# Seven products in another order: a product into another bank between two into the same one

## The chip, the cores and the metric

The kernel runs on one core of a Trainium2 chip. The metric is the device time of one launch in microseconds, lower is better. The kernel before was run three times: median 2225.44 us, from 2217.04 to 2226.3. One further execution was profiled; it took 2224.22 us, of which the profile's span, first to last instruction, is 2222.5 us.

## What is computed

One layer of a causal encoder on 2048 tokens of width 1024, in float32: a gated linear attention mixer (4 heads, keys of 128, values of 256, chunks of 64), then a feed-forward block with a causal convolution of width 3, then a last normalization.

```python
# mixer
h = rmsnorm(x, mix_norm_w)
q, k, v, r, glr = split(h @ gla_w_in, [512, 1024, 2048, 3072])
log_a = log_sigmoid(glr @ w_gate2 + b_gate) / 16
g = cumsum(log_a within a chunk);  k_dec = k * exp(g_end - g)
state = state * exp(g_end) + k_dec^T v        # a scan over 32 chunks
o = q @ state
o = rms_normalize(o) * gla_norm_w * silu(r)
x = x + o @ gla_w_out
# feed-forward
h = rmsnorm(x, ffn_norm_w)
g, val = split(causal_dwconv(h @ ffn_w_up, conv_w, conv_b))
x = x + (silu(g) * val) @ ffn_w_down
out = rmsnorm(x, final_norm_w)
```

Every product is made in three matmuls of a high and a low half (high x low, low x high, high x high), so that float32 accuracy is kept; mm3p (lines 172 to 182) writes these three, at lines 177, 178 and 179.

## The kernel before

The large products are not done block by block but by a Strassen-Winograd scheme: a product of 2 x 2 blocks (two row tiles of 128 tokens, two halves of the inner dimension, two blocks of 512 columns) is made of seven products p1 to p7 of sums and differences of blocks, instead of eight. A product is 4 x 3 = 12 matmuls of 128 x 128 by 128 x 512.

The mixer's projections run as four sweeps over the eight pairs of row tiles, one after another: R (the gate r, and the small gate product glr beside it), A and B (keys, queries and values of heads 0, 1 and of heads 2, 3) and Y (the output projection). One pair in one sweep is a unit (function unit, line 1045). In A and B, and in Y's first two units, the scan of the pairs before runs in between: scan_f, scan_k, scan_o and scan_x are called at fixed places among a unit's 28 quarter products (SLOTS, SLOTS_END, lines 724 to 726). After Y come U, the up projection (phase_u, line 1174) with the order OPS, and D, the down projection (line 1333), with an order of its own.

PSUM has eight banks: four for products (mm_ps, line 124), four for transposes, scan and others (aux_ps, line 127). In a unit, three products begin a bank: p1, p5 and p2. p6, p7 and p4 are added into p1's bank one after another, p3 into p5's. What the bank holds between two of them is also a result: after p1, p5 and p6 ScalarE copies it out (line 1128, tiles cp); after p7, p2 and p3 VectorE adds a copy to it (line 1072, tiles o22, o11, o12); after p4 it is copied out (R, line 1144) or split into halves straight from the bank (A and B, scan_v, line 626). In Y VectorE adds the bank into the residual x after each product (line 1117). A product that is added into a bank can start only when the bank has been read after the product before it.

The weights of a sweep (sums and differences of four blocks of a weight matrix, in high and low halves) lie in seven buffers, one for each product; during the last unit of a sweep each is overwritten with the next sweep's weight, at due times that the kernel keeps on a clock of its own (plan_w, line 326). For A the blocks are loaded into a ring of four raw buffers and added up on VectorE (sum_w, line 286; WPLAN, line 319, gives due times); for B and Y the sums were made and stored before. In Y's last unit the buffers are filled with U's operands instead (load_op, line 882, four loads of 512 KB each on SP's queue). The row operands are split two products ahead (prep_rows, LEAD = 2; tiles h_R, h_A, h_B, h_Y); in R they come from transposed and subtracted blocks in a ring of buffers (hb_tile, line 381; diff, line 384), and R stores them for A and B.

The order is one tuple for sweeps and U alike:

```python
OPS = PORD = ("p1", "p5", "p6", "p7", "p4", "p2", "p3")
```

The code's order is the order of issue that the framework starts from. The framework's scheduler sets the final order of each engine's queue and the semaphores.

Of the kernel before, what the change touches and what calls it, by code (L numbers as in the profile page):

```python
# [10 lines left out]
F32 = mybir.dt.float32  # L11
# [5 lines left out]
P = 128  # L17
# [8 lines left out]
def hybrid_kernel(  # L26
# [17 lines left out]
    nc = tc.nc  # L44
# [11 lines left out]
    NTT = S // P  # L56
# [27 lines left out]
    NS = S // TS  # L84
    TT = TS // P
    PAIRS = TT // 2
    OPS = PORD = ("p1", "p5", "p6", "p7", "p4", "p2", "p3")
    NQ = NF // 2
    ULEAD = 5
    DLEAD = 4  # L90
# [147 lines left out]
    wgot, wload = {}, {}  # L238
# [47 lines left out]
    def sum_w(ps_, o, k):  # L286

        v, r = raws_of(ps_, o, k)
        src = xsum[v]
        if o == "p5":  # L290
            nc.vector.tensor_add(src, *r)
        elif o == "p6":
            nc.vector.tensor_sub(src, src, r[0])
        elif o == "p7":
            nc.vector.tensor_sub(r[1], *r)
        elif o == "p3":
            r = wgot[ps_, "p2", k, (0, 1)]
            nc.vector.tensor_sub(src, r, src)

    def split_w(ps_, o, k):  # L300
        if k == 0:
            t = uh.tile([P, KT, 512], F32R, tag=o, name=f"w_{ps_}_{o}", bufs=1)
            W[ps_, o] = t[:, :HK, :], t[:, HK:, :]
        hi, lo = W[ps_, o]
        if (ps_, o, k) in wgot:
            v, src = (slice(None), slice(2 * k, 2 * k + 2)), wgot[ps_, o, k]
            split(hi[v], lo[v], src)
            if k == 1:
                ready.add((ps_, o))
            return  # L310
        v, r = raws_of(ps_, o, k)
        src = {"p5": xsum[v], "p6": xsum[v], "p3": xsum[v]}.get(o, r[-1] if r else None)
        split(hi[v], lo[v], src)
        if k == 1:
            ready.add((ps_, o))
# [2 lines left out]

    WPLAN = (
# [4 lines left out]
    )  # L324

    def plan_w(ps_):
        def do(o, n):
            if o is None:
                load_w(ps_, n)
                return  # L330
            if o in WSUM:
                sum_w(ps_, o, n)
            split_w(ps_, o, n)

        plan = WPLAN
        if ps_ in "BY":
            plan = [(MADE0 + MADE * m, PORD[m // 2], m % 2) for m in range(2 * len(PORD))]
            for m in range(2 * len(PORD)):
                heapq.heappush(wevents, (clock["now"] + MADE0 + MADE * (m + 0.4), next(seq), lambda m=m: load_made(ps_, m + 1 + RB)))
        for us, o, n in plan:  # L340
            fn = (lambda o=o, n=n: do(o, n)) if ps_ == "A" else (lambda o=o, n=n: split_w(ps_, o, n))
            heapq.heappush(wevents, (clock["now"] + us, next(seq), fn))
        if ps_ == "Y":
            def first_x():
                load_made(ps_, 2 * len(PORD))
                for t in range(2):
                    xin[t] = load_x(t, "x1")

            heapq.heappush(wevents, (clock["now"] + 25.5, next(seq), first_x))
# [15 lines left out]
    rp = {}  # L365
    hsrc = {}
# [12 lines left out]
        nc.vector.scalar_tensor_tensor(xt, xt, rstd, rp["nw"], op0=ALU.mult, op1=ALU.mult)  # L379

    def hb_tile(name):
        return rp["h"].tile([P, 512], F32, tag="hb", name=name, bufs=7)

    def diff(j, o, a, c):
        d = hb_tile(f"ht_{j}_{o}")
        nc.vector.tensor_sub(d, a, c)
        hsrc[j, o] = d
        return d
# [37 lines left out]
    def prep_row(ps_, j, o):  # L426
        if ps_ == "R":
            need(f"h{j}")
            if o == "p4":
                diff(j, o, *hsrc.pop(("p4", j)))  # L430
            split_row(ps_, j, o, hsrc.pop((j, o)))
        else:
            m = jobs.index((ps_, j, o))
            for n in range(m, min(m + HB - 1, len(jobs))):
                if jobs[n] not in hraw:
                    p_, j_, o_ = jobs[n]
                    hraw[jobs[n]] = row_tile(f"hr_{p_}{j_}_{o_}")
                    nc.sync.dma_start(hraw[jobs[n]], (yd if p_ == "Y" else h1d)[j_, o_])
            split_row(ps_, j, o, hraw.pop((ps_, j, o)))
# [181 lines left out]
    def scan_e(g, t):  # L621
        e = sp["a"].tile([P, 2 * DK], F32, tag="E", name=f"E_{g}_{t}", bufs=2)
        nc.sync.dma_start(e, ed[t][:, 2 * g * DK:2 * (g + 1) * DK])
        return e
# [420 lines left out]
    def unit(ps_, j):  # L1045
# [33 lines left out]
        for i, o in enumerate(PORD):  # L1079
# [31 lines left out]
            if ps_ == "Y":  # L1111
                while d not in xin:
                    heapq.heappop(wevents)[-1]()
                xe, xd = xin[e], xin[d]
                for xt, cs in {"p1": ((xe, c1),), "p5": ((xd, c2),), "p6": ((xd, c1),), "p2": ((xe, c1),),
                               "p7": ((xd, c2),), "p3": ((xd, c1),), "p4": ((xe, c2),)}[o]:
                    add(xt[:, cs], xt[:, cs], a)
                if o in ("p2", "p3"):
                    t, xt = (e, xe) if o == "p2" else (d, xd)
                    held.append((t, xt))  # L1120
                if j < 2:
                    scan_slot(4 * i + 4)
                while held and not scan:
                    x1_done(*held.pop(0))
                continue
# [9 lines left out]
            if ps_ == "R":  # L1135
                if o == "p2":
                    nc.sync.dma_start(rd[e][0], o11)
                elif o == "p7":
                    nc.sync.dma_start(rd[d][1], o22)
                elif o == "p3":  # L1140
                    nc.sync.dma_start(rd[d][0], o12)
                elif o == "p4":
                    o21 = out_tile(f"o21_{ps_}_{j}")
                    nc.scalar.copy(o21, a)
                    nc.sync.dma_start(rd[e][1], o21)
            else:
                if o == "p7":
                    if j == 0 and g == 0:
                        scan_a()
                    n = NTT * g + e  # L1150
                    scan[n] = {"g": g, "t": e, "e": scan_e(g, e)}
                    scan[n + 1] = {"g": g, "t": d, "v": scan_v(g, d, o22)}
                elif o == "p4":
                    scan[n]["v"] = scan_v(g, e, a)
                elif o == "p2":
                    if j == 0 and g == 0:
                        scan_b()
                    scan[n]["kq"] = o11
                elif o == "p3":
                    scan[n + 1].update(kq=o12, e=scan_e(g, d))  # L1160
                scan_slot(4 * i + 4)


# [390 lines left out]
```

## Time and profile before

| | |
|---|---|
| median of three runs | 2225.44 us |
| the profiled execution | 2224.22 us, span 2222.5 us |
| granted TensorE clock, mean | 0.986 |
| TensorE matmuls / weight loads | busy 95% / 78% |
| VectorE / ScalarE / GpSimd | busy 74% / 50% / 33% |
| DMA | 411.78 MB, mean 185 GB/s |
| sweep R from 53.6 us, A from 241.2, B from 463.8, Y from 698.8 to 893.7 | 187.6, 222.6, 235.0, 194.9 us |

In the profile a row of a group of instructions names line, engine, operation and tiles (out<-in), and its times. PE is TensorE's matmuls and PEld its weight loads, DVE VectorE, ACT ScalarE, POOL GpSimd, SPq the queue of SyncE that issues most DMAs. The tiles mp_R, mp_A, mp_B and mp_Y are the product banks of the four sweeps. The end of a matmul is modelled, so the distance between starts tells more than the durations.

### The profile page before, as it was taken

What the parts mean: (1) busy time and instruction counts of PE and PEld (TensorE: products, weight loads), DVE (VectorE), ACT (ScalarE), POOL (GpSimd) and SP (SyncE); (2) the same over time, 40 slices, a digit from 0 to 9 for tenths busy, and PEclk for the clock granted to TensorE, in tenths of its full rate; (3) what the DMA queues carried; (4) which work ended last, traced back from release to release, by engine and by line L of the source; (5) the groups of instructions that cost most, each with busy time, mean ns of one, the idle gap of its engine ahead of it and who ended that gap; (6) DMA issues with size and microseconds to landing.
All of it is one profiled execution on the core that took longest, in us unless ns stands there. A gap on an engine that the chain in (4) does not pass through costs nothing.

```text
span 2222.5 us, 29090 instructions
## 1 busy us (share of the span) xinstructions
PE 2122.4 (95%) x9952; PEld 1743.6 (78%) x9952; DVE 1636.5 (74%) x2167; ACT 1107.9 (50%) x2024; POOL 733.1 (33%) x602
## 2 busy tenths in 40 slices
PE   6999999989998999898999999999999999999998
PEld 5888787877887787677887777788888887888886
DVE  8655787789778765488899786897877777457564
ACT  5554755565556676444555453454554443333342
POOL 1000011111111000355566664656555435036100
PEclk9999999999999999999999999999999999999999
DMA  6645684478557889935435348433332468354453
GB/s 210 218 165 182 203 264 157 131 223 299 164 161 235 283 321 352 315 117 174 155 120 193 105 139 288 142 112 102 103 111 85 159 243 289 128 180 152 142 176 113
DMA packets 305125, 411.78 MB, mean 185 GB/s; under 512 B 23742, under 2 KB 160110, under 8 KB 304976
## 3 DMA queue, kind: packets, MB, share of 16 engines
q1 hardware_dynamic: 267440, 346.99, 47.2%
q10 hardware_dynamic: 37536, 62.93, 8.4%
q8 instruction: 78, 1.28, 0.2%
q14 instruction: 71, 0.58, 0.1%
HBM read 266.70 MB, written 143.13 MB: 184 GB/s over the span
## 4 chain that ended last, share of the span: by engine, by line
PE 62%; DVE 14%; DMA 9%; issue 7%; ACT 3%; POOL 3%; SPq 1%; ACTq 0%; DVEq 0%; POOLq 0%
PE ua L177 5%; PE pd_p L178 5%; PE pd_p L179 5%; PE pd_p L177 5%; PE ua L179 5%; PE ua L178 5%; DVE t L1237 4%; PE uc L177 2%; PE uc L179 2%; PE uc L178 2%; PE mp_R L177 2%; PE mp_R L179 2%; PE mp_R L178 2%; PE mp_Y L177 2%; PE mp_Y L179 2%
## 5 line engine op out<-in xcount | busy, mean ns | idle before, releaser
L177 PE MATMUL ua<-h_p,uw_p 128*128 128x512 f32 x704 | 280.2, 398 | 23.6 <-ACT c L1219 23.6
L178 PE MATMUL ua<-h_p,uw_p 128*128 128x512 f32 x704 | 278.6, 396 | 0.0
L179 PE MATMUL ua<-h_p,uw_p 128*128 128x512 f32 x704 | 278.4, 395 | 0.0
L1237 DVE SCALAR_TENSOR_TENSOR t<-u,cw,t 128x1024 f32<-128x1024 f32 x176 | 263.3, 1500 | 8.9 <-ACT t L1235 7.9
L178 PE MATMUL pd_p<-dw_p,da 128*128 128x512 f32 x616 | 240.5, 390 | 3.1 <-DVE da L187 3.1
L179 PE MATMUL pd_p<-dw_p,da 128*128 128x512 f32 x616 | 240.1, 390 | 0.0
L177 PE MATMUL pd_p<-dw_p,da 128*128 128x512 f32 x616 | 240.1, 390 | 0.0
L187 DVE TENSOR_TENSOR uw_p<-ur,uw_p 128x512 fp32r<-128x512 f32 x176 | 168.3, 972 | 58.5 <-ACT uw_p L186 53.3
L187 DVE TENSOR_TENSOR da<-da_p,da 128x512 fp32r<-128x512 f32 x154 | 133.6, 920 | 105.4 <-ACT da L186 105.3
L186 ACT CAST da<-da_p 128x512 fp32r<-128x512 f32 x154 | 85.2, 619 | 208.9 <-PE pd_p L179 153.3
L177 PEld LDWEIGHTS ua<-h_p,uw_p 128*128 128x128 f32 x704 | 134.1, 191 | 57.2 <-ACT c L1219 27.6
L186 ACT CAST uw_p<-us 128x512 fp32r<-128x512 f32 x132 | 82.1, 622 | 165.8 <-POOL us L1199 108.3
L187 DVE TENSOR_TENSOR uw_p<-us,uw_p 128x512 fp32r<-128x512 f32 x132 | 120.4, 921 | 57.6 <-ACT uw_p L186 57.2
L179 PEld LDWEIGHTS ua<-h_p,uw_p 128*128 128x128 f32 x704 | 134.0, 190 | 30.1
L178 PEld LDWEIGHTS ua<-h_p,uw_p 128*128 128x128 f32 x704 | 134.3, 191 | 29.5
L177 PE MATMUL uc<-h_p,uw_p 128*128 128x512 f32 x352 | 138.3, 393 | 1.0 <-DVE t L1237 1.0
L179 PE MATMUL uc<-h_p,uw_p 128*128 128x512 f32 x352 | 138.0, 392 | 0.0
L178 PE MATMUL uc<-h_p,uw_p 128*128 128x512 f32 x352 | 138.0, 392 | 0.0
L178 PEld LDWEIGHTS pd_p<-dw_p,da 128*128 128x128 f32 x616 | 116.0, 188 | 28.0 <-DVE da L187 3.9
L1235 ACT ACTIVATE t<-u,cw 128x1024 f32<-128x1024 f32 x88 | 109.8, 1247 | 51.2 <-DVE u L1328 43.3
L179 PEld LDWEIGHTS pd_p<-dw_p,da 128*128 128x128 f32 x616 | 116.0, 188 | 24.2
L177 PEld LDWEIGHTS pd_p<-dw_p,da 128*128 128x128 f32 x616 | 115.9, 188 | 24.0
(269 smaller groups left out, 5476.2 us busy)
## 6 DMA issues: line engine op xcount, KB each, us to landing
ur<-in_ffn_w_up_dram SPq DMA_DIRECT2D x168, 256.0 KB, 3.7
da_p<-ad_p SPq DMA_DIRECT2D x154, 256.0 KB, 4.1
h_p<-hd_p SPq DMA_DIRECT2D x56, 512.0 KB, 8.1
ad_p<-as_p SPq DMA_DIRECT2D x88, 256.0 KB, 2.7
ad_p<-t SPq DMA_DIRECT2D x66, 256.0 KB, 3.5
x<-in_x_dram SPq DMA_DIRECT2D x32, 512.0 KB, 4.3
ch<-in_ffn_w_down_dram SPq DMA_DIRECT2D x61, 256.0 KB, 4.4
hr_A_p<-h1d_p SPq DMA_DIRECT2D x56, 256.0 KB, 2.7
```

The lines of the kernel that those rows point to most:

```text
L177: nc.tensor.matmul(ps_ap, ah, bl, start=(first and i == 0), stop=False, **kw)
L178: nc.tensor.matmul(ps_ap, al, bh, start=False, stop=False, **kw)
L179: nc.tensor.matmul(ps_ap, ah, bh, start=False, stop=(last and i == len(pairs) - 1), **kw)
L186: nc.scalar.copy(hi, src)
L187: nc.vector.tensor_sub(lo, src, f32(hi))
L1235: nc.scalar.activation(t, u[:, 2:2 + TS], AF.Identity, scale=cw[:, 2, c:c + 1], bias=cw[:, 3, c:c + 1])
L1237: nc.vector.scalar_tensor_tensor(t, u[:, k:k + TS], cw[:, k, c:c + 1], t, op0=ALU.mult, op1=ALU.add)
```

## The change

The sweeps get an order of their own, p1 p5 p6 p2 p7 p3 p4; U keeps the old one. What depended on the order is moved along: p3's weight sum in A is made right after p2's split, and A's due times are set anew; R's difference for p4 is written in place of p2's block, and the ring of blocks gets an eighth buffer; in Y the even tile of a pair is complete after p4 and the odd one after p3; in A and B the scan's entry of the even tile is opened at p2 instead of p7, and the pools that are opened on the way (scan_a, scan_b) open at the fourth and sixth product as before.

```diff
@@ -84,7 +84,9 @@
     NS = S // TS
     TT = TS // P
     PAIRS = TT // 2
-    OPS = PORD = ("p1", "p5", "p6", "p7", "p4", "p2", "p3")
+    OPS = ("p1", "p5", "p6", "p7", "p4", "p2", "p3")
+
+    PORD = ("p1", "p5", "p6", "p2", "p7", "p3", "p4")
     NQ = NF // 2
     ULEAD = 5
     DLEAD = 4
@@ -293,9 +295,8 @@
             nc.vector.tensor_sub(src, src, r[0])
         elif o == "p7":
             nc.vector.tensor_sub(r[1], *r)
-        elif o == "p3":
-            r = wgot[ps_, "p2", k, (0, 1)]
-            nc.vector.tensor_sub(src, r, src)
+        elif o == "p2":
+            nc.vector.tensor_sub(src, r[0], src)
 
     def split_w(ps_, o, k):
         if k == 0:
@@ -318,9 +319,9 @@
 
     WPLAN = (
         (1.0, "p1", 0), (2.5, "p1", 1), (3.5, None, 6), (5.0, "p5", 0), (6.0, None, 8), (9.5, "p5", 1), (10.5, None, 10),
-        (12.0, "p6", 0), (13.0, None, 11), (13.5, "p6", 1), (14.5, None, 12), (17.0, "p7", 0), (18.0, None, 14),
-        (20.0, "p7", 1), (21.0, None, 16), (23.0, "p4", 0), (24.0, "p4", 1), (27.0, "p2", 0), (28.5, "p2", 1),
-        (30.0, "p3", 0), (31.5, "p3", 1),
+        (12.0, "p6", 0), (13.0, None, 11), (13.5, "p6", 1), (14.5, None, 12), (16.5, "p2", 0), (17.5, None, 13),
+        (18.0, "p2", 1), (19.0, None, 14), (21.0, "p7", 0), (22.0, None, 16), (23.5, "p7", 1),
+        (25.0, "p3", 0), (26.5, "p3", 1), (28.0, "p4", 0), (29.0, "p4", 1),
     )
 
     def plan_w(ps_):
@@ -331,6 +332,8 @@
             if o in WSUM:
                 sum_w(ps_, o, n)
             split_w(ps_, o, n)
+            if o == "p2":
+                sum_w(ps_, o, n)
 
         plan = WPLAN
         if ps_ in "BY":
@@ -379,7 +382,7 @@
         nc.vector.scalar_tensor_tensor(xt, xt, rstd, rp["nw"], op0=ALU.mult, op1=ALU.mult)
 
     def hb_tile(name):
-        return rp["h"].tile([P, 512], F32, tag="hb", name=name, bufs=7)
+        return rp["h"].tile([P, 512], F32, tag="hb", name=name, bufs=8)
 
     def diff(j, o, a, c):
         d = hb_tile(f"ht_{j}_{o}")
@@ -427,7 +430,9 @@
         if ps_ == "R":
             need(f"h{j}")
             if o == "p4":
-                diff(j, o, *hsrc.pop(("p4", j)))
+                b21, t2 = hsrc.pop(("p4", j))
+                nc.vector.tensor_sub(b21, b21, t2)
+                hsrc[j, o] = b21
             split_row(ps_, j, o, hsrc.pop((j, o)))
         else:
             m = jobs.index((ps_, j, o))
@@ -1115,8 +1120,8 @@
                 for xt, cs in {"p1": ((xe, c1),), "p5": ((xd, c2),), "p6": ((xd, c1),), "p2": ((xe, c1),),
                                "p7": ((xd, c2),), "p3": ((xd, c1),), "p4": ((xe, c2),)}[o]:
                     add(xt[:, cs], xt[:, cs], a)
-                if o in ("p2", "p3"):
-                    t, xt = (e, xe) if o == "p2" else (d, xd)
+                if o in ("p3", "p4"):
+                    t, xt = (e, xe) if o == "p4" else (d, xd)
                     held.append((t, xt))
                 if j < 2:
                     scan_slot(4 * i + 4)
@@ -1144,20 +1149,19 @@
                     nc.scalar.copy(o21, a)
                     nc.sync.dma_start(rd[e][1], o21)
             else:
-                if o == "p7":
+                n = NTT * g + e
+                if o == "p2":
                     if j == 0 and g == 0:
                         scan_a()
-                    n = NTT * g + e
-                    scan[n] = {"g": g, "t": e, "e": scan_e(g, e)}
+                    scan[n] = {"g": g, "t": e, "e": scan_e(g, e), "kq": o11}
+                elif o == "p7":
                     scan[n + 1] = {"g": g, "t": d, "v": scan_v(g, d, o22)}
+                elif o == "p3":
+                    if j == 0 and g == 0:
+                        scan_b()
+                    scan[n + 1].update(kq=o12, e=scan_e(g, d))
                 elif o == "p4":
                     scan[n]["v"] = scan_v(g, e, a)
-                elif o == "p2":
-                    if j == 0 and g == 0:
-                        scan_b()
-                    scan[n]["kq"] = o11
-                elif o == "p3":
-                    scan[n + 1].update(kq=o12, e=scan_e(g, d))
                 scan_slot(4 * i + 4)
```

## The prediction

> **What bounds the kernel now.** I read the page first: the span, and the share of TensorE.
>
> ```profile
> span 2222.5 us, 29090 instructions
> PE 2122.4 (95%) x9952; PEld 1743.6 (78%) x9952; DVE 1636.5 (74%) x2167; ACT 1107.9 (50%) x2024; POOL 733.1 (33%) x602
> ```
>
> TensorE is the bound, so only its lost time counts. The four sweeps take the first 890 us; next I read the busy time by stretch, cut where R, A, B and Y begin and end (length, then busy us of PE, PEld, DVE, ACT, POOL; last clock, DMA share, GB/s).
>
> ```profile
> 53.60:241.20 187.60, 186.51 (x1101) 153.60 (x1101) 118.76 (x179) 96.48 (x174) 8.52 (x11) 1.00 0.57 193
> 241.20:463.80 222.60, 213.60 (x1121) 179.58 (x1119) 175.77 (x318) 135.95 (x293) 29.54 (x35) 0.99 0.57 188
> 463.80:698.80 235.00, 220.30 (x1154) 184.94 (x1153) 195.25 (x361) 134.03 (x302) 37.90 (x33) 0.98 0.65 210
> 698.80:893.70 194.90, 182.71 (x865) 148.90 (x864) 131.86 (x225) 127.72 (x281) 18.41 (x22) 0.97 0.89 312
> ```
>
> Two things to keep: VectorE is busy 79% of A and 83% of B, and Y moves data at a DMA share of 0.89. Idle time in the matmul rows understates a stall, because a matmul is recorded some 0.39 us long while the next starts 0.23 us after it (B's unit below: from 634.23 to 636.88 there are eleven steps); so the waits are read from the weight loads (PEld), in the view of waits, one answer for each sweep (us in total, times, longest).
>
> ```profile
> PEld mp_R L177 <- ACT cp_R L1128: 1.6, 6, 0.3
> ...
> PEld mp_R L177 <- DVE o_R L1072: 1.1, 4, 0.3
> PEld mp_A L177 <- ACT cp_A L1128: 8.5, 7, 4.3
> ...
> PEld mp_A L177 <- DVE o_A L1072: 1.3, 2, 0.9
> PEld mp_B L177 <- ACT cp_B L1128: 4.6, 8, 1.1
> PEld mp_B L177 <- DVE o_B L1072: 4.6, 5, 1.0
> PEld mp_Y L177 <- DVE x L1117: 7.3, 12, 1.2
> ```
>
> These are the bank turns: p7 adds into the bank that p6 filled and waits for its copy (L1128), p4 into the bank of p7 and waits for the addition that reads it (L1072); in Y both wait for an addition at L1117. One unit of B, in order of time:
>
> ```profile
> 628.46 0.48 PE L177 MATMUL mp_B<-w_B_p,h_B_p 128*128 128x512 f32 x1
> 629.09 0.50 PE L177 MATMUL mp_B<-w_B_p,h_B_p 128*128 128x512 f32 x1
> 629.42 0.39 PE L178 MATMUL mp_B<-w_B_p,h_B_p 128*128 128x512 f32 x1
> ...
> 633.25 0.28 PE L178 MATMUL po<-sh,q 128*128 128x256 f32 x1
> 634.23 0.50 PE L177 MATMUL mp_B<-w_B_p,h_B_p 128*128 128x512 f32 x1 [0.70 <-DVE o_B L1072]
> ...
> 636.88 0.40 PE L179 MATMUL mp_B<-w_B_p,h_B_p 128*128 128x512 f32 x1
> ```
>
> A product begins with L177, then L178, so two L177 in a row are two products: at 628.46 the first matmul of p2 had been put ahead of p7, which starts at 629.09. The framework's scheduler thus already fills these waits with work for other banks, here with one matmul of p2 and later with matmuls of the scan (po). The written order is therefore not the order that runs, and only what it left open can be won: 629.09 - 628.46 - 0.23 = 0.40 us before p7, and before p4 0.70 us by the idle time of its own row. In Y there is less to fill in with:
>
> ```profile
> 836.11 0.39 PE L179 MATMUL mp_Y<-w_Y_p,h_Y_p 128*128 128x512 f32 x1
> 837.28 0.50 PE L177 MATMUL mp_Y<-w_Y_p,h_Y_p 128*128 128x512 f32 x1 [0.78 <-DVE x L1117]
> ```
>
> which is 1.17 - 0.23 = 0.94 us.
>
> **What the change removes.** With p1 p5 p6 p2 p7 p3 p4, each of p7 and p4 has a whole product into another bank ahead of it: 12 matmuls of 0.227 us, 2.72 us, against turns of at most 1.2 us in a unit after the first. From the waits above, without the one of 4.3 us in A: R 2.7, A 8.5 - 4.3 + 1.3 = 5.5, B 9.2, Y 7.3, together 24.7 us in 43 waits. A weight load takes 188 ns of a step of 0.227 us, so a gap of 0.04 is normal:
>
> ```profile
> L178 PEld LDWEIGHTS mp_R<-w_R_p,h_R_p x196: 186/188/192, 53.7 to 240.1; 128*128 128x128 f32 x196
> ```
>
> Thus 43 x 0.04 = 1.7 us of it is no loss; but the matmul after a wait is followed 0.33 us later (629.09 to 629.42) and not 0.23, which adds 43 x 0.107 = 4.6. Bank turns: 24.7 - 1.7 + 4.6 = 27.6 us.
>
> The wait of 4.3 us lies in A's first unit:
>
> ```profile
> 250.31 0.40 PE L179 MATMUL mp_A<-w_A_p,h_A_p 128*128 128x512 f32 x1
> 254.57 0.53 PE L177 MATMUL mp_A<-w_A_p,h_A_p 128*128 128x512 f32 x1 [3.86 <-ACT cp_A L1128]
> 254.91 0.62 PE L178 MATMUL mp_A<-w_A_p,h_A_p 128*128 128x512 f32 x1
> ...
> 258.31 0.40 PE L177 MATMUL mp_A<-w_A_p,h_A_p 128*128 128x512 f32 x1
> ```
>
> On the other engines meanwhile:
>
> ```profile
> 250.44 1.23 DVE L298 TENSOR_TENSOR xsum<-wr_A,xsum 128x1024 f32<-128x1024 f32 x1 [4.23 <-DMA wr_A<-in_gla_w_in_dram]
> 253.90 0.62 ACT L1128 COPY cp_A<-mp_A 128x512 f32<-128x512 f32 x1
> ```
>
> ScalarE copies p6 only at 253.90, behind casts and gate work. With p2 in between, 2.72 us of that wait is worked through; p2's weight now comes in ahead of p7's four raw halves, and the addition at L298, which held VectorE 4.23 us for p2's weight, gets its data earlier. After the wait eight further matmuls start 0.425 us apart (254.91 to 258.31), 8 x 0.2 = 1.6 us, while after the short wait in B the steps are 0.23 us again (634.23 to 636.88). I take 2.7 + 1.6 = 4.3 us; the bounds are -4.3 (p7's halves, now a product later in the ring of four buffers, make a wait as long at p7 or p4) and +5.9 (all of it goes).
> [...]
>
> Gross gain: 27.6 + 4.3 = 31.9 us.
>
> **What it adds and moves.** No instruction is added; the same products, copies and additions run. The costs are waits in new places.
>
> (a) VectorE in A and B. One undisturbed unit of B, and the split that frees p4's bank:
>
> ```profile
> 616.71:644.38 27.67, 26.82 (x148) 22.77 (x146) 21.55 (x44) 15.27 (x37) 4.66 (x5) 1.00 0.50 162
> 637.94 0.69 DVE L187 TENSOR_TENSOR vl<-mp_B,vh 128x512 fp32r<-128x512 f32 x1 [2.38 <-ACT vh L186]
> ```
>
> 21.55 of 27.67 us are work; at 26.3 us a unit that is 82% in place of 78%. It is an in-order queue, so some of what TensorE wins it will wait for later, at row splits or in the scan. A and B hold 5.5 + 9.2 = 14.7 of the 24.7 us, so 16.4 of the 27.6. Between 0 and 16.4 I take 4: the 2.38 us in which VectorE itself waited for p4 show that it is not behind.
>
> (b) Y runs on transfers at 0.89. Its part is 7.3/24.7 of 27.6, 8.2 us; 194.9 - 8.2 would need a share of 0.93, which the chip gives in Y's own end (below). Between 0 and 8.2 I take 2.5.
>
> (c) The start of U. In Y's last unit each product is followed by four loads into the buffer that its weight leaves (load_op, on SP's queue), and U still uses them as p1 p5 p6 p7 p4 p2 p3. p7's loads move from fourth to fifth, p4's from fifth to last, behind p7's, p2's and p3's.
>
> ```profile
> 873.48 46.93 SPq L886 DMA_DIRECT2D h_p<-hd_p  x28
> h_p<-hd_p SPq DMA_DIRECT2D x28, 512.0 KB, 8.7
> 900.00:920.00 20.00, 12.79 (x63) 9.66 (x61) 2.93 (x5) 11.46 (x28) 4.77 (x8) 1.00 1.04 382
> 919.93 0.50 PE L177 MATMUL ua<-h_p,uw_p 128*128 128x512 f32 x1 [4.78 <-ACT c L1219]
> ```
>
> The 28 issues end at 920.41 and the last lands 8.7 us later, at 929.1, with the DMA engines full (1.04). p7 starts at 919.93, and two products of it make p4 due at 926 to 928. So p4 waits 1 to 3 us, and if Y's gain doesn't pull the loads forward, up to 8 more. Between 0 and 10 I take 3. The stores and loads that move with the products in R and A (o11's store, the E loads) stay on SP's queue at shares of 0.57, ahead of nothing that is due.
>
> (d) R takes four banks a unit (p1, the gate sums, p5, p2) of four. If they rotate strictly, p1 of the next unit gets the bank of p4, now the product just before it: 7 turns of Y's 0.94 us, 6.6 us. If any free bank is taken, p2's is free long before and it costs nothing, and the gate matmuls after p1, which write another bank, can be put in between besides. Between 0 and 6.6 I take 1. The p4 difference of R (VectorE, one 128x512) is made two products later and in place; its row is split two products ahead as before, so it is hidden.
>
> (e) The last unit of one sweep and the first of the next are held by VectorE making weights:
>
> ```profile
> 700.00:720.00 20.00, 13.14 (x61) 10.29 (x60) 17.99 (x32) 14.36 (x28) 3.04 (x3) 0.81 0.75 245
> ```
>
> 18 of 20 us there are VectorE's. About 1 us of turn in each of three last units isn't won, and first units may lose it too: between 0 and 5, I take 2.
>
> Sum: 31.9 - 4 - 2.5 - 3 - 1 - 2 = 19.4 us. The profiled execution took 2224.22 us, its span 2222.5, so 2205; it lies 1.2 us under the median of 2225.44, and the runs spread from 2217.04 to 2226.3.
>
> **The rivals.** First: VectorE becomes the bound in A and B, (a) at 16.4. For it speak its 83% in B, against it that it waits 2.38 us for p4. Then 31.9 - 16.4 - 8.5 = 7 us, 2217. Second: the transfers take it, (b) at 8.2 and (c) at 10, so 31.9 - 18.2 - 7 = 6.7 us, 2217.5; for it the 1.04 after Y, against it that A and B, at 0.57 and 0.65, aren't touched. Third, the change doesn't do what it says: the scheduler, which already reorders, ends with as many turns as it has now: 2224. Fourth, slower: p4, now last, frees its bank in A and B only after a cast and the split by VectorE. Today the split ends at 638.63 and p4's last matmul at 636.88 + 0.40 = 637.28: a lag of 1.35 us, under the 2.72 us of the next unit's p1, after which p5 wants a bank. It decides once VectorE comes so late that the lag passes 2.72; at 4.8 us each of 16 units pays 2.1, 33 us, so 2205 + 33 = 2238. Against it: the lag would have to grow by 3.4 us.
>
> **How the numbers follow.** The forecast (15 to 28 us faster about) 0.63; VectorE 0.13; transfers 0.10; no effect 0.05; slower 0.09. Under about 0.5%, 11 us, a measurement of this kernel can't be told from no change. The second to fourth fall within that, so faster 0.64, same 0.26, slower 0.10, with the last's neighbours counted in. All costs at their least give 2224 - 33.5 = 2191, all at their most about 2245; cutting a tenth on each side leaves 2194 to 2221.
>
> **What would show it.** In the waits of the weight loads, the rows from cp_R, cp_A, cp_B, o_R, o_A, o_B and x together fall from 29 us to under 6; B's undisturbed unit of 27.67 us takes 26 to 26.6; Y is shorter by 5 to 8 us. Right for (c) is a wait of TensorE for h_p, or a gap of over a microsecond ahead of p4, before 935 less what was won; for (d) rows of o_R L1144 ahead of mp_R. I am wrong if A and B keep their 222.6 and 235.0 us although the turns are gone (first rival), or if vl's split ends more than 2.7 us after p4 (fourth).

## The result, and the profile after

The changed kernel takes 2188.8 us (median of four runs, 2186.47 to 2190.18), the kernel before beside it 2224.31 us (2217.04 to 2226.3): a ratio of 0.9849, 95% interval 0.9832 to 0.9866, so 35.5 us less. The prediction of 2205, range 2194 to 2221, had the sign right and little more than half of the size. The profiled execution took 2187.85 us.

The page of the changed kernel, its span and engine rows:

```profile
span 2186.1 us, 29137 instructions
PE 2106.7 (96%) x9952; PEld 1741.1 (80%) x9952; DVE 1636.7 (75%) x2167; ACT 1106.0 (51%) x2024; POOL 728.4 (33%) x602
```

The busy time by stretch of the changed kernel, cut where R, A, B and Y begin and end (length, busy us of PE, PEld, DVE, ACT, POOL, then clock, DMA share, GB/s):

```profile
53.80:238.30 184.50, 183.84 (x1102) 154.12 (x1101) 119.96 (x180) 98.27 (x176) 6.77 (x11) 1.00 0.59 198
238.30:447.90 209.60, 208.86 (x1118) 177.76 (x1116) 172.12 (x316) 131.60 (x286) 30.14 (x35) 1.00 0.61 197
447.90:668.70 220.80, 214.42 (x1154) 182.51 (x1153) 192.58 (x361) 133.16 (x304) 37.51 (x33) 0.99 0.67 225
668.70:862.20 193.50, 182.31 (x866) 150.69 (x865) 130.85 (x226) 128.72 (x286) 18.21 (x23) 0.96 0.91 319
```

Against the rows of before, R gained 187.6 - 184.5 = 3.1 us, A 222.6 - 209.6 = 13.0, B 235.0 - 220.8 = 14.2, Y 194.9 - 193.5 = 1.4. That is 31.7 of the spans' 36.4 us; the other 4.7 came after Y. VectorE is now busy 82% of A and 87% of B, which shows that more than 83% was to be had.

The waits of the weight loads of the changed kernel, one answer for each sweep (us in total, times, longest; line 177 is now 179, 1128 is 1133, 1117 is 1122):

```profile
PEld mp_A L179 <- ACT cp_A L1133: 1.3, 2, 0.9
...
PEld mp_B L180 <- DVE h_B_p L189: 2.8, 3, 1.7
PEld po L179 <- DVE sl L189: 2.7, 1, 2.7
PEld mp_B L179 <- ACT cp_B L1133: 2.0, 2, 1.6
...
PEld pt_d L793 <- ACT h L784: 4.8, 3, 3.6
PEld px L723 <- DVE og L715: 4.4, 1, 4.4
...
PEld mp_Y L179 <- DVE x L1122: 0.2, 1, 0.2
```

The bank rows, 29 us before, are down to 1.3 + 2.0 + 0.2 = 3.5 us. R's rows name none, and no wait names the row that R copies out after p4. (One turn is hidden there: p4 of R's last unit starts at 235.46; the addition that frees its bank ran until 235.31, behind weight work, and the row names ScalarE's w_A_p, which ended 0.1 us later.) One undisturbed unit of B:

```profile
590.30:616.50 26.20, 26.20 (x146) 22.69 (x145) 21.75 (x45) 15.02 (x38) 4.34 (x4) 1.00 0.53 171
```

It takes 26.20 us for 27.67, and PE counts as busy for all of it. Unit by unit (from the start of its first matmul to that of the next unit, worked out from the starts in the trace):

| | units 1 to 8 of the sweep, us |
|---|---|
| A before | 30.2, 26.7, 27.9, 29.2, 27.6, 26.9, 26.9, 26.9 |
| A after | 26.2, 24.9, 26.6, 27.5, 26.2, 26.2, 26.2, 25.7 |
| B before | 39.7, 28.2, 29.8, 27.7, 27.7, 27.7, 27.7, 26.7 |
| B after | 32.4, 30.6, 27.1, 26.2, 26.2, 26.2, 26.2, 25.8 |
| Y before | 41.4, 21.5, 22.3, 21.2, 21.2, 21.9, 22.1, 23.4 |
| Y after | 38.5, 22.5, 20.8, 21.6, 20.9, 21.2, 20.9, 27.2 |

Three things are to be seen. The undisturbed units gained 0.7 us (A) and 1.4 us (B) each. B's first unit alone gained 7.3. And Y gained 5.2 in its first seven units and lost 3.8 in the last.

I also added up, matmul by matmul, by how much each start lay later than the usual step of its kind, and put each excess down to what ended just before it. Bank turns in the four sweeps went from 22.7 to 3.4 us (R 1.2 to 0.8, A 8.7 to 0.7, B 8.2 to 1.5, Y 4.6 to 0.4), the many small excesses of at most 0.15 us from 21.2 to 18.0, and everything else, waits for inputs and slow matmuls, from 33.9 to 25.2. Together that is 31.2 of the 31.7 us. The split depends somewhat on what is taken as the usual step: with the median of each kind the three differences come to about 20, 4 and 8 us.

### The profile page after: what moved, and what is told of

Its sections match the earlier page's. It is cut to its first block, busy times and chain, and to the rows that moved or that the text cites. A ratio compares the mean times of both kernels' runs of the same rounds, so it can differ in the third digit from the quotient of the medians.

```text
span 2186.1 us, 29137 instructions
## 1 busy us (share of the span) xinstructions
PE 2106.7 (96%) x9952; PEld 1741.1 (80%) x9952; DVE 1636.7 (75%) x2167; ACT 1106.0 (51%) x2024; POOL 728.4 (33%) x602
## 4 chain that ended last, share of the span: by engine, by line
PE 68%; DVE 13%; DMA 7%; issue 5%; ACT 3%; POOL 2%; SPq 1%; ACTq 0%; DVEq 0%; POOLq 0%
PE ua L179 5%; PE pd_p L180 5%; PE pd_p L181 5%; PE pd_p L179 5%; PE ua L180 5%; PE ua L181 5%; DVE t L1241 4%; PE mp_R L179 2%; PE uc L179 2%; PE uc L180 2%; PE uc L181 2%; PE mp_R L181 2%; PE mp_R L180 2%; PE mp_A L179 2%; PE mp_A L181 2%
## 5 line engine op out<-in xcount | busy, mean ns | idle before, releaser
L180 PE MATMUL ua<-h_p,uw_p 128*128 128x512 f32 x704 | 278.9, 396 | 0.0
L180 PE MATMUL pd_p<-dw_p,da 128*128 128x512 f32 x616 | 239.9, 389 | 2.6 <-DVE da L189 2.6
L181 PEld LDWEIGHTS ua<-h_p,uw_p 128*128 128x128 f32 x704 | 134.2, 191 | 29.9
L180 PEld LDWEIGHTS ua<-h_p,uw_p 128*128 128x128 f32 x704 | 134.3, 191 | 29.5
L180 PE MATMUL uc<-h_p,uw_p 128*128 128x512 f32 x352 | 138.0, 392 | 0.0
L180 PEld LDWEIGHTS pd_p<-dw_p,da 128*128 128x128 f32 x616 | 115.6, 188 | 27.3 <-DVE da L189 3.4
L666 POOL TENSOR_TENSOR r<-r,gnw 128x512 f32<-128x512 f32 x32 | 48.3, 1508 | 263.4 <-ACT r L665 226.3
L181 PEld LDWEIGHTS pd_p<-dw_p,da 128*128 128x128 f32 x616 | 115.6, 188 | 23.9
```

The costliest lines, as they stand in the source:

```text
L180: nc.tensor.matmul(ps_ap, al, bh, start=False, stop=False, **kw)
L181: nc.tensor.matmul(ps_ap, ah, bh, start=False, stop=(last and i == len(pairs) - 1), **kw)
L666: nc.gpsimd.tensor_mul(r, r, sp["gnw"])
```

## The experiments

In short diffs `-` is the changed kernel, unless said otherwise, and `+` the experiment. What depends on the order (due times, the scan's entries) is moved along with it. Medians are of all runs; stretches, units and waits are from the one profiled execution of each kernel. Lines shift by one or two between kernels; in those with an order for each sweep, L180 to L182 are the three matmuls of a product and L1078 is the addition that reads a bank.

**Which sweeps.** The new order in A and B alone, and in R and Y alone.

```diff
-    PORD = ("p1", "p5", "p6", "p2", "p7", "p3", "p4")
+    NEW, OLD = ("p1", "p5", "p6", "p2", "p7", "p3", "p4"), OPS
+    PORDS = {"R": OLD, "A": NEW, "B": NEW, "Y": OLD}   # ab_only
+    PORDS = {"R": NEW, "A": OLD, "B": OLD, "Y": NEW}   # ry_only
```

> The new order in sweeps A and B alone, the old one in R and Y. By the stretches of the two traces A and B are 27.3 us shorter of 36.4. Theory (each sweep's gain is its own): A and B take 210 and 221 us as in the changed kernel, the whole 2195 to 2200. Rival (part of A's and B's gain is R's or Y's order, through rows, weights or data that arrive earlier): A and B stay over 435 us together, the whole over 2203.

> The new order in R and Y alone, the old one in A and B. Theory: R 3 us shorter, Y and U's first group together 3 to 6 us, the whole 2214 to 2219. Rival: Y's gain is given back at U's start, because p4's loads come last: U's first group longer than 50 us and no gain of Y and U together.

A and B alone: 2199.14 us, 0.99 (0.9871 to 0.9928), 23 us under the 2222.28 before. R and Y alone: 2213.19 us, 0.9957 (0.9942 to 0.9972), 9 us. The sum, 32, is nearly the whole 35. B's first unit takes 32.4 us with the new order in A and B and 38.6 without it, so that gain belongs to A and B themselves, or to the clock that they get there (see (e) below). A's first unit stays at 30.2 and 29.9 us in both and is 26.2 only when R has the new order too: its 4 us belong to neither half. With the new order in them alone A and B took 216.3 + 224.0 = 440.3 us, not 430.4 as in the changed kernel. That is over the 435 that was to speak for the rival (the profiled execution was the slowest of the four, 2208.2 us), so a part of their gain does need R's or Y's order.

**Is VectorE the bound in A and B?** Three row splits of each unit but the first make their low half twice, the same subtraction into the same tile, 1.8 us more of VectorE a unit.

```diff
         split(t[:, 0, :], t[:, 1, :], src)
+        if ps_ in "AB" and j and o in ("p1", "p6", "p7"):
+            nc.vector.tensor_sub(t[:, 1, :], src, f32(t[:, 0, :]))
```

> The changed kernel with three of a unit's seven row splits subtracted twice on VectorE in A and B (units after the first): 3 x 0.6 = 1.8 us more VectorE work in a unit of 26.2, 14 units. Theory (VectorE has room, TensorE is the bound): under 0.4 us a unit, the whole 2188 to 2194. Rival (VectorE is the bound of A and B now): 1.8 us a unit, 2209 to 2214.

2192.26 us, 0.986 (0.9844 to 0.9877): 3.5 us more than the changed kernel, for 14 x 1.8 = 25 us of added work. The undisturbed units stay at 26.2 us; what was lost lies in A's and B's units beside weight work (A 211.8 us, B 225.6, together 7.0 us longer in the trace). That is 0.5 us a unit for 1.8 us of work: VectorE has room there, and the first rival falls.

**Only one of the two turns parted.** p2 between p6 and p7 alone, or between p7 and p4 alone.

```diff
-    PORD = ("p1", "p5", "p6", "p2", "p7", "p3", "p4")
+    PORD = ("p1", "p5", "p6", "p2", "p7", "p4", "p3")   # part_p6p7
+    PORD = ("p1", "p5", "p6", "p7", "p2", "p4", "p3")   # part_p7p4
```

> Order p1 p5 p6 p2 p7 p4 p3 in all four sweeps: only the turn from p6 to p7 is parted, p4 still follows p7 into the same bank. Theory (the gain is the bank turns, each for itself): in the waits before the change the turn p6 to p7 holds the cp rows of R, A and B (1.6 + 4.2 + 4.6 us), nearly all of Y's 7.3 and the 4.3 us of A's first unit, with slow restarts some 23 us of the 32 that I counted, so about two thirds to three quarters of the measured 35 us: 2224 - 23 to 27 = 2197 to 2201. Rival (only the full order gives it, or it is luck of the schedule): the gain is under 10 us or as large as the full one.

> Order p1 p5 p6 p7 p2 p4 p3: only the turn from p7 to p4 is parted, p7 still follows p6. Theory: the o rows of R, A and B (1.1 + 1.3 + 4.6 us) and their restarts, some 8 to 12 us: 2212 to 2216. With the run before it the two add up to the 35 us of the full order. Rival: as in the run before.

2219.14 us, 0.999 (0.9977 to 1.0003), and 2219.62 us, 0.999 (0.9975 to 1.0004), beside 2220.19. Each alone is worth nothing that can be told, and both together 35 us. In undisturbed units of B the parts do add: 27.7 before, 27.2 and 26.7 with one parted, 26.2 with both. The gain is lost elsewhere. Bank turns in all came to 25.7 and 24.6 us in place of 22.7, because the turn that was left had grown. The clearest place is R, which had 1.2 us of turns. The waits of its weight loads with p6 and p7 parted:

```profile
PEld mp_R L180 <- DVE o_R L1078: 6.8, 4, 2.1
```

One of the four, TensorE and VectorE in the same kernel, in order of time:

```profile
125.35 0.39 PE L182 MATMUL mp_R<-w_R_p,h_R_p 128*128 128x512 f32 x1
125.58 0.40 PE L180 MATMUL mp_R<-w_R_p,h_R_p 128*128 128x512 f32 x1
...
126.51 0.39 PE L181 MATMUL mp_R<-w_R_p,h_R_p 128*128 128x512 f32 x1
127.98 0.50 PE L180 MATMUL mp_R<-w_R_p,h_R_p 128*128 128x512 f32 x1 [1.09 <-DVE o_R L1078]
```

```profile
125.45 1.28 DVE L406 COPY hb<-pt_a 128x512 f32<-128x512 f32 x2
126.65 0.68 DVE L390 TENSOR_TENSOR ht_p<-hb,hb 128x512 f32<-128x512 f32 x1
127.25 0.68 DVE L1078 TENSOR_TENSOR o_R<-mp_R,cp_R 128x512 f32<-128x512 f32 x1
```

p7 ends at 125.35 + 0.39 = 125.74. The scheduler has put five matmuls of p3 (125.58 to 126.51) into the wait for p4, but VectorE makes two copies and a difference for coming rows before the addition that frees the bank, so p4 starts 1.47 us after the last of the five. Before, with transposes and gate work in that place, the weight loads waited at most 0.3 us for such an addition in R. A is alike: one turn of 3.32 us there has row splits, the decayed keys and a weight sum ahead of the addition.

**Are the reads what counts?** p6's copy and p7's addition made twice, in the order before and in the new one (R, A, B).

```diff
                 nc.scalar.copy(keep[o], a)
+                if o == "p6":
+                    nc.scalar.copy(keep[o], a)
...
                 o22 = out(a, keep["p5"], "o22")
+                add(o22, a, keep["p5"])
```

> The kernel before with the two reads made longer that the turns wait for: p6's copy out of the bank is done twice (ScalarE, 0.59 us more) and p7's addition twice (VectorE, 0.68 us more) in R, A and B; the result is the same. Theory: the turns wait for these reads, so 23 units lose up to 1.1 us each, less what the scheduler fills: 2236 to 2250. Rival (TensorE waits for something else): under 5 us more.

> The same doubling in the changed kernel. Theory: the 2.72 us of a product cover the longer read, 2188 to 2193. Rival: VectorE or ScalarE have become the bound, and it loses as much as the kernel before, 2200 to 2215.

In the order before: 2221.09 us, 0.9993 (0.9977 to 1.0009). In the new order: 2204.77 us, 0.992 (0.9892 to 0.9947), 16 us more than the changed kernel. That is the reverse of what a longer turn should do. In the order before, the scheduler seems to put more work of other banks into the waits: undisturbed units of B even come to 27.0 us in place of 27.7, the bank rows of A and B shrink, and other rows of the weight loads take their place (order before with double reads, A and B):

```profile
PEld po L177 <- DVE sl L187: 13.0, 15, 2.8
PEld pd L566 <- DVE ll L187: 6.9, 1, 6.9
```

In the new order the profiled execution, the fastest of the four, has a span 11.0 us longer than that of the changed kernel, and R alone is 11.3 us longer (195.8 for 184.5). There p4 waits for the doubled addition (new order with double reads, R):

```profile
PEld mp_R L179 <- DVE o_R L1140: 9.5, 4, 3.7
```

So in R one product in between did not cover the doubled addition and what stands ahead of it in VectorE's queue; in A and B, 434.0 us together for 430.4, it mostly did.

**Do weight sums on VectorE hold up the turn that is left?** In A and B VectorE also adds up blocks for B and Y, 16 additions of 1.22 us. R has none of them: in the changed kernel they start between 291.9 and 324.7 and between 487.5 and 520.4 us. First they were moved to GpSimd, in all four orders.

```diff
-        steps_ = (("p5", nc.vector.tensor_add, a22, a21, a22), ("p7", nc.vector.tensor_sub, a21, a11, a21),
-                  ("p6", nc.vector.tensor_sub, a11, a22, a11), ("p3", nc.vector.tensor_sub, a12, a12, a11))
+        steps_ = (("p5", nc.gpsimd.tensor_add, a22, a21, a22), ("p7", nc.gpsimd.tensor_sub, a21, a11, a21),
+                  ("p6", nc.gpsimd.tensor_sub, a11, a22, a11), ("p3", nc.gpsimd.tensor_sub, a12, a12, a11))
```

> The order p1 p5 p6 p2 p7 p4 p3 (only p6 to p7 parted), with the 16 additions that make the next sweep's weight sums in A and B (make_sums, 1.22 us each on VectorE) put on GpSimd. In the run without this the turn from p7 to p4, left as it was, took 3.3 and 2.0 us in A and 1.5, 2.8 and 2.2 us in B in the units where VectorE makes these sums, and 0.6 to 0.8 us in the undisturbed ones. Theory (a turn costs what VectorE is late with the read): they fall to under 1.2 us, and the whole to 2209 to 2214. Rival (they are late for another reason): no change, 2217 to 2221.

> The same for the order p1 p5 p6 p7 p2 p4 p3 (only p7 to p4 parted). Without it p4 waited 2.7, 2.6 and 3.3 us for p7's reader in the units with sums, though p2 stands between. Theory: these go, the turns from p6 to p7 of 0.46 us stay, the whole 2209 to 2214. Rival: no change, 2217 to 2221.

> The changed kernel with the same sums on GpSimd. It has no late turn in these units, so the theory gives little: VectorE's lateness shows only as 1 to 3 us in rows and scan, 2185 to 2190. Rival (VectorE still holds A and B): 2175 to 2183.

> The kernel before with the same sums on GpSimd, the control for the first two. Its turns in the units with sums were filled by the scheduler with p2 and the scan and took 0.4 to 1.1 us. Theory: 1 to 4 us faster, 2217 to 2221. Rival (VectorE held A and B before): as much as the parted orders win, 2209 to 2213.

All four were slower than without the move: 2238.82 (1.0067, 1.0045 to 1.0089), 2230.47 (1.0024, 1.0007 to 1.0041), 2209.44 (0.9929, 0.9905 to 0.9953) and 2232.7 us (1.0049, 1.003 to 1.0068). The test was spoilt by a cost of its own. GpSimd with the changed order:

```profile
280.85 2.62 POOL L278 TENSOR_TENSOR wm_B<-wm_B,wm_B 128x1024 f32<-128x1024 f32 x1 [9.48 <-DMA wm_B<-in_gla_w_in_dram]
284.58 0.71 POOL L712 TENSOR_TENSOR rstd<-var,neghalf 128x2 f32<-128x2 f32 x1 [1.10 <-DVE var L711]
287.36 7.45 POOL L278 TENSOR_TENSOR wm_B<-wm_B,wm_B 128x1024 f32<-128x1024 f32 x3 [2.07 <-DMA wm_B<-in_gla_w_in_dram]
```

An addition takes about 2.5 us there and waits for its load, and the scan's rstd (L712) stands behind in the same queue; A alone grew from 209.6 to 222.9 us with the changed order, and its third unit, where these additions lie, from 26.6 to 41.0. So the additions were left out instead: the loaded blocks are stored as they are, and the projections work on other weights.

```diff
         def step(o, fn, dst, x, y):
-            fn(dst, x, y)
             nc.sync.dma_start(wsd[ps_, o, k], dst)
```

> The kernel before, with one thing left out: the 16 additions that make the weight sums for B and Y (VectorE, 128x1024 each, 1.2 us) aren't made; the loaded blocks are stored as they are, so all transfers are kept and the projections of B and Y work on other weights. First theory (these additions stand before the bank additions in VectorE's queue and make bank turns longer in R, A and B): faster than before by 1 to 6 us, 2218 to 2223. Rival (they cost TensorE nothing): 2224.

> Order p1 p5 p6 p2 p7 p4 p3 in the four sweeps, only p6 and p7 parted, and the same 16 additions left out. First theory (a single parting gained nothing because the turn that it leaves, without work to fill it, waits for a VectorE held by these additions): now the parting is worth something, 2205 to 2212, 8 to 15 us under the kernel before with the additions left out. Rival (what eats the gain of a single parting is the lost filling alone, whatever VectorE does): within 4 us of the kernel before with the additions left out.

> Order p1 p5 p6 p7 p2 p4 p3, only p7 and p4 parted, and the same 16 additions left out. First theory: 2205 to 2214, 6 to 15 us under the kernel before with the additions left out. The turn that is left waits for ScalarE's copy of p6, which these additions reach only through the row splits, so this one may gain less of it than the other. Rival (lost filling alone): within 4 us.

> The changed kernel with the same 16 additions left out. Both turns are parted, so both theories expect little: 2183 to 2189, 0 to 6 us under the changed kernel. Were it much faster (2175), the additions would cost TensorE by another way, at row splits or in the scan.

2225.48 us (1.0018, 1.0006 to 1.003), 2218.36 (0.9983, 0.997 to 0.9997), 2219.62 (0.9989, 0.9976 to 1.0001) and 2188.67 (0.9847, 0.9831 to 0.9864). Beside the kernel before with the additions left out, the single partings are 7 and 6 us ahead, which lies between what the two theories expect; beside the same orders with their additions they gained 0.8 and 0. With p6 and p7 parted the turns of A and B, by the starts, came to 14.6 us without the additions and 16.1 with them, and R's, which these additions don't touch, to 5.8 us again. The theory that these additions are what holds the turn falls: 20 us of VectorE work less bought next to nothing. R's own weight sums for A (L299) were not left out in any run.

**Is it ScalarE, standing at a load?** With p6 and p7 parted ScalarE stood 19.6 us in 17 waits at the load of r (16.2 us in the changed kernel), with row casts behind it, VectorE at those rows, and the bank's addition behind them. The gate's activation was moved a slot later, for the new order and for p6 and p7 parted alone.

```diff
         nc.sync.dma_start(r, rd[t][g])
-        nc.scalar.activation(r, r, AF.Silu)
-        nc.gpsimd.tensor_mul(r, r, sp["gnw"])
...
         g, t, v = (scan[n][k] for k in ("g", "t", "v"))
+        r = scan[n]["r"]
+        nc.scalar.activation(r, r, AF.Silu)
+        nc.gpsimd.tensor_mul(r, r, sp["gnw"])
```

> The changed kernel with the gate's activation (ScalarE, the Silu of r right behind the issue of r's load, on which ScalarE waits up to 3.6 us, 16.2 us in all in A, B and Y) and the product after it made a slot later, at the start of the scan's key step, when r is long there. Theory (ScalarE, standing at r's load, holds up row splits, and VectorE behind them the bank additions): a little faster than the changed kernel, 2180 to 2187, since both turns are parted and only the longest stalls show through; A's third unit and B's second, 26.6 and 30.6 us, come nearer to 26.2. Rival (the stalls come from elsewhere): 2187 to 2191.

> Order p1 p5 p6 p2 p7 p4 p3, with the gate's activation a slot later as in the run beside it. Theory (in the units where the scan runs beside weight work, the turn that is left lies behind that stall): A's units 2 and 3 and B's units 1 to 3, 31.2, 28.3, 30.2, 30.6 and 30.1 us with this order, come down to 27 to 28, and the time to 2205 to 2213. Rival (the turn left waits for other reasons): 2215 to 2221, units as before.

2187.55 us (0.9848, 0.9824 to 0.9872), no different from the changed kernel, and 2216.07 us (0.9976, 0.9963 to 0.9989), some 3 us better than the same order without the move, though the intervals overlap. The stand at r's load was lessened, not removed: from 19.6 to 11.5 us with p6 and p7 parted, from 16.2 to 10.4 in the new order. B's units 3 and 4 came from 30.6 and 30.1 to 29.3 and 27.1 us, A's unit 4 from 28.3 to 26.7; A's unit 3 went from 31.2 to 33.1. So it is a part of the loss at most, as far as the move took the stand away.

**Y's last unit.** It lost 3.8 us though its turns are gone. ScalarE of the changed kernel, then TensorE:

```profile
837.77 0.18 ACT L207 ACTIVATION_READ_ACCUMULATOR h<-x 128x1 f32 x1
840.96 0.37 ACTq L1190 DMA_DIRECT2D ur<-in_ffn_w_up_dram  x1
841.44 1.15 ACT L784 ACTIVATE h<-x,rstd_d 128x1024 f32<-128x1024 f32 x1 [3.48 <-issue]
```

```profile
839.04 0.40 PE L181 MATMUL mp_Y<-w_Y_p,h_Y_p 128*128 128x512 f32 x1
842.64 1.97 PE L793 MATMUL pt_d<-ident,h 128*128 128x128 f32 x8 [3.21 <-ACT h L784]
```

ScalarE does nothing from 837.95 until its own queue issues the fifth of U's first eight weight loads at 840.96; the normalization that TensorE transposes stands behind it. To test that, these eight loads were issued on SP's queue.

```diff
-            q = nc.scalar if s == 0 and g == 0 else nc.sync
+            q = nc.sync
```

> The changed kernel with U's first eight weight loads issued on SP's queue and not on ScalarE's. In the trace of the changed kernel ScalarE stood 3.48 us behind the issue of one of these loads in Y's last unit, and TensorE behind ScalarE's row for a transpose. Theory: Y's last unit of 27 us falls to 22 to 23, and the whole by 3 to 6 us, 2183 to 2186. Rival: the loads now come late behind the 28 loads on SP's queue and U's first group loses as much: 2188 to 2196.

2187.37 us, 0.9842 (0.9828 to 0.9857). Y came to 190.0 us and its last unit to 22.7, so the issue on ScalarE's queue started the loss. The wait is the smaller part of it. In the changed kernel the granted clock was 0.5 from 841.9, still in the wait, to 848.7. In the run with three splits made twice, TensorE waits the same 3.21 us in the same place, has steps of 0.23 us after it, and the unit takes 24.3 us in place of 27.2. So 2.8 of the 3.8 us were slow matmuls, which followed this wait in one execution and not in the other (lines in the last section).

But U's first group of units took 57.1 us in place of 47.7 and its second 42.9 in place of 47.1. TensorE of that kernel:

```profile
871.65 0.80 PE L179 MATMUL uc<-h_p,uw_p 128*128 128x512 f32 x1 [9.20 <-ACT uw_p L188]
```

On SP's queue the first of U's weight loads after 838 us was issued at 859.4 (at 841.0 on ScalarE's queue in the changed kernel), and TensorE stood 9.20 us for a weight made of such loads. The stall was had in Y or in U; the sum is the same within 2 us.

## Why the prediction was right and wrong

The mechanism was right and the size was not. The sum failed in two of its steps: the deductions took away 12.5 us for waits in new places, of which only a loss in Y's last unit was seen, for another reason, and other waits had no term for growing shorter, which gave 11.6 us. Even with all costs at their least the sum ended at 2191, over the 2188.8 measured.

**What bounds, and the gross.** Right in kind. The bank rows fell from 29 to 3.5 us (forecast: under 6), B's undisturbed unit took 26.20 us (forecast: 26 to 26.6), and A's first unit gained 4.0 us (forecast: 4.3). In size the gross of 31.9 us was too high for the bank turns as such: by the starts in the trace they, the small excesses (the restarts among them) and the slow matmuls of A's first unit gave 19.3 + 3.2 + 1.8 = 24.3 us. The step that read them from the weight loads overstated Y most: 7.3 us less the normal gaps is 6.8, against 4.2 by the starts. Seven of Y's twelve waits were of this kind, in the kernel before:

```profile
794.46 0.39 PE L179 MATMUL mp_Y<-w_Y_p,h_Y_p 128*128 128x512 f32 x1
794.46 0.19 PEld L177 LDWEIGHTS mp_Y<-w_Y_p,h_Y_p 128*128 128x128 f32 x1
794.94 0.19 PEld L177 LDWEIGHTS mp_Y<-w_Y_p,h_Y_p 128*128 128x128 f32 x1 [0.30 <-DVE x L1117]
```

The load waits 0.30 us, but the loads beside it start some 0.23 us ahead of their matmuls, and this one starts with its own. That matmul begins at 794.94 by the trace, 0.26 us after the one before it: 0.03 us are lost, not 0.30. R's waits, none over 0.31 us, are much alike.

The 1.6 us of the gross for slow matmuls in A's first unit were the author's estimate that none would be left there; no run shows how short a wait must be for that. The starts gave the 1.8 us above, and the granted clock in that unit of the changed kernel is 1.00 (0.94 before).

**The deductions are the step that failed.** 31.9 - 4 - 2.5 - 3 - 1 - 2 took 12.5 us away for waits in new places. In the sweeps other waits became shorter instead of longer, by 8.7 us, or 6.9 without the 1.8 just counted, and the stretch after Y by 4.7 us. So the forecast of 19.4 us against the spans' 36.4 comes apart as - 7.6 (gross) + 12.5 (deductions) + 6.9 + 4.7, with 0.5 not placed. The gross was 7.6 us too high by a misreading, which by luck hid as much of the rest. Term by term:

(a) VectorE, 4 us: nothing of it was seen in the undisturbed units. VectorE at 82 to 87% made the same units of 26.2 us with 1.8 us more on top. The argument that 2.38 us of slack show it not to be behind was right and should have set the term to zero.

(b) Y, 2.5 us: Y lost 6.8 of the 8.2 us allowed it, more than forecast and for another reason. About half of the loss is the gross that was overstated; the other half, 3.8 us, lies in the last unit: the wait behind the issue on ScalarE's queue, and for 2.8 us the slow matmuls after it; with the loads on SP the unit took 22.7 us. (The row that the prediction calls Y's own end, 900 to 920, lies after Y, in U.) The DMA share did reach 0.91, but no row of the waits shows TensorE waiting for the transfers of Y's own operands beyond 1.7 us.

(c) The start of U, 3 us: no wait for h_p appears, and U's first group took 47.7 us for 49.9. Of the 4.7 us after Y this is 2.2; the rest of it is no more than what that stretch moves between the runs here (1319 to 1329 us), and I leave it unexplained.

(d) Strict rotation of R's banks, 1 us: no row shows it. The one late release in the changed kernel (A's last unit: vl is split at 457.44, 10 us after p4) did not stop the p5 of the next unit, which in strict rotation would get the same bank and starts at 450, so a free bank is taken out of turn. With that the fourth rival falls too; the second falls by the start of U, the third by the bank rows.

(e) First and last units, 2 us: wrong in sign. B's first unit gained 7.3 us. Its waits before and after, the weight loads in that unit:

```profile
PEld px L718 <- DVE og L710: 2.7, 1, 2.7
PEld mp_B L178 <- DVE h_B_p L187: 1.7, 1, 1.7
PEld pq L652 <- DVE o_B L1072: 1.5, 1, 1.5
PEld po L177 <- DVE sl L187: 1.5, 1, 1.5
PEld px L718 <- issue: 1.4, 1, 1.4
PEld mp_B L177 <- ACT cp_B L1128: 0.5, 1, 0.5
```

```profile
PEld mp_B L180 <- DVE h_B_p L189: 2.8, 3, 1.7
PEld mp_B L179 <- ACT cp_B L1133: 1.6, 1, 1.6
PEld px L723 <- DVE og L715: 0.8, 2, 0.6
PEld pk L685 <- ACT kz L188: 0.6, 1, 0.6
PEld px L723 <- issue: 0.6, 1, 0.6
```

Only 0.5 us of the old waits was a bank turn. The rows come to 9.3 us before and 6.4 after: waits of the scan for VectorE (og, sl, o_B) went, which the prediction had no term for. About as much is the clock, in the same unit before and after:

```profile
463.80:503.50 39.70, 32.16 (x152) 26.07 (x150) 32.57 (x54) 23.47 (x47) 6.34 (x6) 0.87 0.67 212
447.80:480.20 32.40, 28.82 (x151) 22.89 (x151) 30.12 (x52) 24.16 (x51) 6.23 (x5) 1.00 0.70 225
```

Before, the granted clock was 0.5 for 10.2 us of it and the slow matmuls cost 3.4 us by their starts; after, there are none. The run with p6 and p7 parted alone has 35.1 us there with 3.4 us at half clock, the one with p7 and p4 parted 39.6 with 10.2. So most of it comes with p2's place ahead of p7; by which way was not tested.

**What stays open.** Why each parting alone is worth nothing is located, not settled. The turn that is left grows in R, in A's and B's units beside weight work and in Y's last unit, and there VectorE's queue holds row work ahead of the addition. Of two suspected reasons, the weight sums for B and Y were taken away and ScalarE's stand at r's load was lessened by some 8 us; that gave back at most 3 us. The clock has a share. In the traces it was granted at 0.5 for 23.9 us of the four sweeps before and 17.1 after, but for 31.7 and 37.5 with one turn parted. Counted as the excess of the steps in these stretches, slow matmuls cost 8.0, 6.6, 12.6 and 14.7 us. So with one turn parted slow matmuls took 4.6 and 6.7 us more than before, beside the waits themselves. These are single executions, and no run held the clock fixed. That the scheduler has less to put into the turn that is left, and that it takes VectorE to be earlier than it is, fits R's rows, but no run changed that alone. A version that beats the changed kernel was not found: late gate work (2187.55) and loads on SP (2187.37) are no different from it.

## What to carry to other kernels

Here what one of two waits in a unit cost depended on the other: parting either alone gave 0.999, parting both 0.985, so try the complete change before giving up on a half that shows nothing. A deduction for a wait in a new place needs a row that shows the engine behind; here rows showed slack (2.38 us on VectorE), the deductions stood all the same, and they were the largest part of the error. When work is pulled ahead, look at the issues of DMAs on compute engines' queues at the next stage's start: one such issue, with the slow matmuls behind the wait, took 3.8 us back.

## What the runs showed of the hardware

Slow matmuls followed idle times shorter than the 3.86 us in A's first unit of the kernel before. With p6 and p7 parted alone, TensorE in Y's last unit:

```profile
880.74 0.39 PE L182 MATMUL mp_Y<-w_Y_p,h_Y_p 128*128 128x512 f32 x1
883.56 0.77 PE L180 MATMUL mp_Y<-w_Y_p,h_Y_p 128*128 128x512 f32 x1 [2.43 <-DVE x L1123]
884.12 0.63 PE L181 MATMUL mp_Y<-w_Y_p,h_Y_p 128*128 128x512 f32 x1
884.55 0.63 PE L182 MATMUL mp_Y<-w_Y_p,h_Y_p 128*128 128x512 f32 x1
```

After 2.43 us of idle the first step is 0.56 us and the next is 0.43, with a granted clock of 0.5 from 883.5 to 886.9. A longer wait came in Y's last unit of the changed kernel (842.64, shown above) and of the run with three splits made twice. What follows it, first in the one and then in the other:

```profile
844.84 0.63 PE L180 MATMUL mp_Y<-w_Y_p,h_Y_p 128*128 128x512 f32 x1
845.26 0.63 PE L181 MATMUL mp_Y<-w_Y_p,h_Y_p 128*128 128x512 f32 x1
```

```profile
848.56 1.09 PE L795 MATMUL pt_d<-ident,h 128*128 128x128 f32 x8 [3.21 <-ACT h L786]
...
849.74 0.40 PE L180 MATMUL mp_Y<-w_Y_p,h_Y_p 128*128 128x512 f32 x1
849.97 0.40 PE L181 MATMUL mp_Y<-w_Y_p,h_Y_p 128*128 128x512 f32 x1
```

The same 3.21 us of idle are followed by steps of 0.42 us in one and 0.23 us in the other. Nor did the slow steps begin at once everywhere: in A of the run with p6 and p7 parted a wait of 3.16 us ends at 319.35, the next steps have the usual length, and only then is the clock 0.5 from 320.3 to 323.7.

So in these traces the length of a gap alone does not tell whether slow matmuls follow: 3.21 us had both outcomes, and 2.43 us were enough in one case.
